# Where VectorE's and GpSimd's instructions stand in a stretch of 128 slots: a rotary embedding kernel

## The chip, the cores and the metric

The kernel runs on one core of one Trainium2 chip. The metric is device time in microseconds for one launch. Three runs gave a median of 163.52 us (163.49 to 163.62). One more execution was taken by the hardware profiler, and all durations below come from that one.

A core has five engines, each with its own stream of instructions: TensorE (PE in the profile; its weight loads are PEld), VectorE (DVE), ScalarE (ACT), GpSimd (POOL) and SyncE (SP). Data moves between the main memory (HBM) and the on-chip memory by 16 DMA engines. In this kernel SP and ACT issue the data transfers; each transfer is split over all 16 DMA engines. The engines' own instructions are also fetched from HBM by these DMA engines; the profile lists such fetches as a queue of kind "instruction".

## The reference

`x` has the shape 8 x 2048 x 8 x 64 (batch, position, head, features), in float32. `cos` and `sin` have one row of 32 values for each position.

```python
x1 = x[..., : x.shape[-1] // 2]
x2 = x[..., x.shape[-1] // 2 :]
out1 = x1 * cos - x2 * sin
out2 = x1 * sin + x2 * cos
return np.concatenate([out1, out2], axis=-1)
```

The input has 33.55 MB and so has the output; each is moved once.

## The kernel before

**Tiling.** A batch is one tile `xt` of 128 partitions with 8192 floats each (16 positions of 512 floats for each partition; 4 MB). Five such tiles exist (`NBUF`), and a result is written into the tile that its input came from. A batch is worked off in pieces of 2048 floats for each partition (`UNIT`); the first and the last batch have some pieces of 1024.

**The work on a piece.** `rotate` knows three kinds. Kind A, most of them: GpSimd makes `t2`, which is x with its halves exchanged, times `sin` for one half and times `-sin` for the other (two instructions, L124); VectorE makes `t1` = x times `cos` (L131) and adds the two into `xt` (L138). In kinds B and C, five pieces in all, TensorE adds by multiplying with a unit matrix `eye` (or its negative `neye`), and ScalarE copies the sum from PSUM into `xt` (L147, L167); in kind C VectorE also does GpSimd's multiplication (L150).

**Transfers.** SP issues the loads of `x` and `cos` (L67, L69) and the stores of the last batch; ACT issues the load of `sin` (L76) and the other stores (L74). The first batch comes in three loads: 1 MB, 1 MB and 2 MB. Five batches are requested at the start; batch b + 5 is requested when batch b has been worked off, and waits for the store that frees the tile.

**The start.** Every engine has a fixed opening of the runtime, then a common barrier. After it VectorE's first own instruction is the copy of `cos` into PSUM (L95), which waits for `cos`. GpSimd's first are a memset and a select that build `eye` (L82, L83); its first multiplication (L124) waits for `sin` and for the first load of `x`. ACT makes `nsin`, the negative of `sin`, the copy `sin_ps` and `neye` (L92 to L94).

**Slots.** An instruction takes one slot of 64 bytes, so 128 slots are 8192 bytes, the size of each larger fetch in the trace. `addr_align(128, offset=k)` is no instruction of the engine: when the program is loaded, it is replaced by as many padding slots as bring the next instruction onto slot k of a stretch of 128. By default the engine walks through the padding, which is empty instructions (NOP); with `max_nops=0` the first padding slot is a jump to the aligned instruction. `keep` fixes an instruction's place in the engine's order. The two calls stand behind the loads and ahead of the building of `eye`. VectorE's 107 instructions from L95 to its last sum (waits that stand alone included) and GpSimd's 78 from L82 to its last product follow.

Of the kernel before, what the change touches and what calls it, by code (L numbers as in the profile page):

```python
# [10 lines left out]
def kernel(  # L11
# [7 lines left out]
    nc = tc.nc  # L19
    keep = tc.keep_in_program_order  # L20
# [56 lines left out]
    for b in range(NBUF):  # L77
        load(b)

    keep(nc.vector.addr_align(128))  # L80
    keep(nc.gpsimd.addr_align(128, offset=120))
    keep(nc.gpsimd.memset(eye, 0.0))  # L82
    nc.gpsimd.affine_select(  # L83
        out=eye,
# [141 lines left out]
```

## Time and profile before

| | |
|---|---|
| median of three runs | 163.52 us (163.49 to 163.62) |
| profiled execution: its own time | 163.48 us |
| profiled execution: span from the first to the last instruction of the program | 161.7 us |
| VectorE busy | 140.1 us, 87% |
| GpSimd busy | 138.8 us, 86% |
| TensorE, ScalarE busy | 49.6 us, 12.8 us |
| moved by DMA | 67.65 MB, 418 GB/s over the span |
| fetches of instructions in the span | 2 |

Times in all views count from the first instruction of the program. What lies between the span and the execution's own time, 1.8 us, is mostly the runtime's closing work. Busy time of an engine excludes the instructions that only wait, branch, pad or issue transfers. A "releaser" is what ended an idle stretch of an engine.

### The profile page before, as it was taken

The numbers are of one execution on the slowest core, as the hardware profiler recorded it, in microseconds if no ns is written. First come the engines' busy times: TensorE is split into PE (matmuls) and PEld (weight loads), VectorE is DVE, ScalarE is ACT, GpSimd is POOL, SyncE is SP. The second block draws the span as 40 slices with busy tenths as digits, with TensorE's granted clock in tenths as the row PEclk, the third lists the DMA queues.
The fourth block names the chain that finished last, engine by engine and source line by source line (L and its number), as shares of the span: only waits on it lengthen the run. The fifth ranks groups of instructions, "written<-read, shape, count | busy, mean of one in ns | idle before, by whom it ended". The sixth has DMA issues, their size and how long they took to land.

```text
span 161.7 us, 573 instructions
## 1 busy us (share of the span) xinstructions
PE 49.6 (31%) x80; PEld 18.7 (12%) x80; DVE 140.1 (87%) x66; ACT 12.8 (8%) x14; POOL 138.8 (86%) x70
## 2 busy tenths in 40 slices
PE   0000000597309760978049723973000000000000
PEld 0000000142004220322023302320000000000000
DVE  0297999999999999999999999199989999899950
ACT  3300000002200220021100220022000000000000
POOL 1399994999999999992999979999799997999800
PEclk9999999999975998589956995599655555555555
DMA  5999999999999999999999999999999999999995
GB/s 184 418 432 438 420 428 405 444 409 489 397 401 450 438 462 397 438 462 397 438 462 397 438 462 397 438 470 389 438 470 389 438 470 397 430 470 397 405 420 213
DMA packets 3458, 67.65 MB, mean 418 GB/s; under 512 B 384, under 2 KB 384, under 8 KB 768
## 3 DMA queue, kind: packets, MB, share of 16 engines
q1 hardware_dynamic: 2016, 38.01, 55.4%
q10 hardware_dynamic: 1440, 29.62, 42.7%
q14 instruction: 2, 0.02, 0.0%
HBM read 34.08 MB, written 33.55 MB: 418 GB/s over the span
## 4 chain that ended last, share of the span: by engine, by line
DMA 48%; DVE 37%; POOL 9%; issue 2%; DVEq 0%; SPq 0%; POOLq 0%; ACTq 0%
DMA xt<-in_x_dram 26%; DMA out_dram<-xt 19%; DVE t L131 18%; DVE xt L138 17%; POOL t L124 9%; DMA sin_sb<-in_sin_dram 4%; DVE t L150 1%; DVEq L138 0%; SPq L67 0%; POOLq L124 0%; ACTq L74 0%
## 5 line engine op out<-in xcount | busy, mean ns | idle before, releaser
L124 POOL TENSOR_TENSOR t<-xt,sin_sb 128x1024 f32<-128x1024 f32 (+1 forms) x32 | 70.5, 2203 | 11.3 <-DMA xt<-in_x_dram 5.2
L131 DVE TENSOR_TENSOR t<-xt,cos_ps 128x2048 f32<-128x2048 f32 (+1 forms) x34 | 73.4, 2167 | 0.8
L124 POOL TENSOR_TENSOR t<-xt,nsin 128x1024 f32<-128x1024 f32 (+1 forms) x32 | 70.5, 2202 | 0.0
L138 DVE TENSOR_TENSOR xt<-t,t 128x2048 f32<-128x2048 f32 (+1 forms) x29 | 62.2, 2145 | 8.0 <-POOL t L124 5.4
L145 PE MATMUL o<-t,eye 128*128 128x512 f32 x24 | 17.2, 807 | 22.9 <-DVE t L131 19.5
L162 PE MATMUL o<-t,eye 128*128 128x512 f32 x16 | 12.1, 847 | 37.7 <-DVE t L131 35.5
L146 PE MATMUL o<-t,eye 128*128 128x512 f32 x24 | 14.9, 709 | 0.0
L147 ACT COPY xt<-o 128x1024 f32<-128x1024 f32 x6 | 6.1, 1012 | 45.7 <-PE o L146 45.7
L145 PEld LDWEIGHTS o<-t,eye 128*128 128x128 f32 x24 | 5.6, 257 | 32.3 <-issue 26.4
L162 PEld LDWEIGHTS o<-t,eye 128*128 128x128 f32 x16 | 3.7, 256 | 43.1 <-issue 39.3
L167 ACT COPY xt<-o 128x1024 f32<-128x1024 f32 x4 | 4.0, 1012 | 47.8 <-PE o L163 36.8
L95 DVE COPY cos_ps<-cos_sb 128x512 f32<-128x512 f32 x1 | 0.7, 695 | 6.9 <-DMA cos_sb<-in_cos_dram 6.9
L146 PEld LDWEIGHTS o<-t,eye 128*128 128x128 f32 x24 | 5.7, 239 | 8.2 <-issue 7.7
L163 PE MATMUL o<-t,neye 128*128 128x512 f32 x8 | 6.3, 882 | 0.2 <-DVE t L150 0.2
L150 DVE TENSOR_TENSOR t<-xt,sin_ps 128x2048 f32<-128x2048 f32 x2 | 4.6, 2281 | 0.0
L163 PE MATMUL o<-t,eye 128*128 128x512 f32 x8 | 4.1, 592 | 0.0
L163 PEld LDWEIGHTS o<-t,neye 128*128 128x128 f32 x8 | 2.2, 306 | 5.3 <-issue 3.7
L82 POOL MEMSET eye<- 128x128 f32 x1 | 0.2, 204 | 2.4 <-issue 2.4
L163 PEld LDWEIGHTS o<-t,eye 128*128 128x128 f32 x8 | 1.5, 190 | 1.9 <-issue 1.9
L92 ACT ACT_TABLE_LOAD x1 | 1.3, 1283 | 1.2 <-PEq L210 1.2
L92 ACT ACTIVATE nsin<-sin_sb 128x512 f32<-128x512 f32 x1 | 0.6, 629 | 4.0 <-DMA sin_sb<-in_sin_dram 4.0
L93 ACT COPY sin_ps<-sin_sb 128x512 f32<-128x512 f32 x1 | 0.6, 579 | 0.0
(6 smaller groups left out, 1.0 us busy)
## 6 DMA issues: line engine op xcount, KB each, us to landing
xt<-in_x_dram SPq DMA_DIRECT2D x7, 4096.0 KB, 41.4
out_dram<-xt ACTq DMA_DIRECT2D x6, 4096.0 KB, 28.6
xt<-in_x_dram SPq DMA_DIRECT2D x2, 1024.0 KB, 6.9
xt<-in_x_dram SPq DMA_DIRECT2D x1, 2048.0 KB, 13.1
out_dram<-xt ACTq DMA_DIRECT2D x1, 2048.0 KB, 25.8
out_dram<-xt SPq DMA_DIRECT2D x1, 2048.0 KB, 10.0
out_dram<-xt SPq DMA_DIRECT2D x2, 1024.0 KB, 6.3
out_dram<-xt ACTq DMA_DIRECT2D x1, 1536.0 KB, 20.7
```

Source lines behind the costliest of these rows:

```text
L92: keep(nc.scalar.mul(nsin, sin_sb, -1.0))
L95: keep(nc.vector.tensor_copy(cos_ps, cos_sb))
L124: nc.gpsimd.tensor_mul(out=t2u[:, :, u, :].rearrange("p (r h) d -> p r h d", h=H), in0=xu[:, :, 1 - u, :].rearrange("p (r h) d -> p r h d" ...
L131: nc.vector.tensor_mul(out=t1.rearrange("p (r k d) -> p r k d", r=nr, d=Dh), in0=xk, in1=rep(cos_ps[:, r0 : r0 + nr, :], 2 * H),)
L138: keep(nc.vector.tensor_add(out=xt, in0=t1, in1=t2))
L145: nc.tensor.matmul(oc, eye, t1[:, cs], start=True, stop=False)
L146: nc.tensor.matmul(oc, eye, t2[:, cs], start=False, stop=True)
L147: keep(nc.scalar.copy(xt[:, 2 * j * C : 2 * (j + 1) * C], o))
L150: nc.vector.tensor_mul(out=t2.rearrange("p (r k d) -> p r k d", r=nr, d=Dh), in0=xk, in1=rep(sin_ps[:, r0 : r0 + nr, :], 2 * H),)
L162: nc.tensor.matmul(oc, eye, t1u[:, gs, u, :], start=True, stop=False)
L163: nc.tensor.matmul(oc, eye if u else neye, t2u[:, gs, 1 - u, :], start=False, stop=True)
L167: nc.scalar.copy(xu[:, :, u, :], o.rearrange("p (g d) -> p g d", d=Dh))
```

## The change

VectorE's and GpSimd's alignment both become slot 8 of a stretch, with a jump in place of the padding's empty instructions. Before, VectorE's copy of `cos` stood on slot 0 and GpSimd's memset of `eye` on slot 120 of a stretch. Nothing else of the program differs: all five engines have the same instructions in the same order with the same waits.

```diff
-    keep(nc.vector.addr_align(128))
-    keep(nc.gpsimd.addr_align(128, offset=120))
+    for eng in (nc.vector, nc.gpsimd):
+        keep(eng.addr_align(128, offset=8, max_nops=0))
     keep(nc.gpsimd.memset(eye, 0.0))
```

## The prediction

> **What bounds the kernel now.** I read the strips of the page first, then a table by stages, then how the run ends.
>
> ```profile
> DVE  0297999999999999999999999199989999899950
> ...
> POOL 1399994999999999992999979999799997999800
> ...
> DMA  5999999999999999999999999999999999999995
> ```
>
> VectorE and GpSimd look full, but each has slices of 1 to 7 tenths; the DMA strip has none between its ends. The table by stages (columns: stretch, its length, busy time of PE, PEld, DVE, ACT, POOL, clock, share of the 16 DMA engines, GB/s) says the same in numbers: from 2 us on the share is 0.96 to 1.02.
>
> ```profile
> 0.00:2.00 2.00, 0.00 (x0) 0.00 (x0) 0.00 (x0) 0.84 (x1) 0.20 (x4) 1.00 0.31 49
> 2.00:8.00 6.00, 0.00 (x0) 0.00 (x0) 1.06 (x2) 1.80 (x4) 2.00 (x4) 1.00 0.96 381
> 8.00:16.00 8.00, 0.00 (x0) 0.00 (x0) 6.84 (x6) 0.00 (x0) 8.00 (x6) 1.00 1.02 434
> ...
> 120.00:158.00 38.00, 0.00 (x0) 0.00 (x0) 34.25 (x17) 0.00 (x0) 31.77 (x16) 0.50 0.99 425
> ```
>
> The trace also records every packet. On one DMA engine a packet starts 3 ns before the one ahead of it ends, so 16 chains of packets can be followed from 1.75 us to the end; they hardly have a hole. They end between 159.41 and 160.50 us. The last store shows it from outside: its 1 MB would take 2.5 us at 424 GB/s (16 packets of 32 KB in 1.213 us each, the usual row), but it was issued at 155.86 and landed at 160.83, 5.0 us later, behind the store before it. So the end is set by the DMA engine that has the most to do. A transfer counts as landed when its slowest DMA engine is through, so one late engine makes everything late, and time of VectorE or GpSimd is worth nothing unless the DMA engines run dry.
>
> **What the padding costs now.** These are the padding and what follows it on both engines.
>
> ```profile
> L80 DVEq NOP  x61: 18/18/18, 0.8 to 3.6; - x61
> L81 POOLq NOP  x52: 13/13/13, 0.7 to 2.7; - x52
> ```
> ```profile
> 2.81 0.20 POOL L82 MEMSET eye<- 128x128 f32 x1 [2.37 <-issue]
> 3.09 0.29 POOL L83 TENSOR_SCALAR_AFFINE_SELECT eye<-eye 128x128 f32<-128x128 f32 x1
> ...
> 6.49 1.26 POOL L124 TENSOR_TENSOR t<-xt,sin_sb 128x512 f32<-128x512 f32 x1 [3.11 <-DMA sin_sb<-in_sin_dram]
> 6.91 0.69 DVE L95 COPY cos_ps<-cos_sb 128x512 f32<-128x512 f32 x1 [6.91 <-DMA cos_sb<-in_cos_dram]
> ...
> 7.49 0.30 ACT L94 ACTIVATE neye<-eye 128x128 f32<-128x128 f32 x1
> ```
>
> VectorE walks 61 slots from 0.76 to 3.62 us (47 ns each), GpSimd 52 from 0.69 to 2.77 us (40 ns each). That is 2.86 and 2.08 us, and none of it counts: VectorE then waits until 6.91 for `cos`, GpSimd until 6.49 for `sin` (3.11 us of waiting left), and `eye`, complete at 3.39, is first read at 7.49, when ACT reaches it. `cos` and `sin` were requested by SP and ACT at 1.17 and 0.73, which wait for neither padding. So taking the empty instructions out: 0. The jump that replaces them has no row here. Its cost is bounded by nothing and by 3.1 us, GpSimd's remaining wait, before it could show; the nearest row is a padding slot, 0.04 to 0.05 us. I take 0. [...]
>
> **What moves: the fetches.** Counting the padding back, VectorE's first padding slot was slot 67 (128 - 61) and GpSimd's 68 (120 - 52). Before, VectorE walks into the next stretch at 3.6 us, with the copy of `cos` on its slot 0. GpSimd has memset, a register move, two configurations, select, one wait and two multiplications on slots 120 to 127, and goes over with its third multiplication. After, both jump there at about 0.75 us and stand on slot 8. From there VectorE's 107 instructions end at slot 114 and GpSimd's 78 at slot 85, so neither crosses again in the program. The two fetches of the page fit these two crossings:
>
> ```profile
> q14 instruction: 2, 0.02, 0.0%
> ```
>
> The packet records put them at 7.688 and 10.466 us, 8192 bytes and 309 ns each, on two DMA engines. Neither came out free: the next packet on the first of these chains took 924 ns where its neighbours take 309, on the second 926 where they take 611. So they cost their DMA engines 0.309 + 0.615 = 0.92 and 0.309 + 0.315 = 0.62 us. The landings show what that does to everyone. Of the 16 parts of the first three loads the last landed 0.13 to 0.15 us after the last but one. Of the second load of `x` (the first one that a fetch hit) it was 0.64, of the third 0.45, and of the last five stores 0.46, 0.42, 0.47, 0.48 and 0.47. The chains end the same way: the last three at 159.999, 160.047 and 160.501. Chains that run in step can be confused in following them, so that the last one is the engine hit at 7.688 is inferred from this steady lag, not read.
>
> What a fetch costs when it comes elsewhere: if it is through before the chains begin at 1.75 us, nothing; inside the stream, 0.62 to 0.92 by the two rows above.
>
> When will they come? VectorE stood on slot 0 from 3.6 to 6.9 us and no fetch came; one came 0.8 us after the copy was released. So the fetch follows not arriving in a stretch but having moved a slot or a few into it. GpSimd got past its first two slots at about 7.15 us (after `nsin` at 7.08) and past the next two at 10.0 (the second load); with 7.688 for VectorE and 10.466 for GpSimd the fetch comes 0.4 to 0.8 us after slot 1 to 3. If what counts is how far into the stretch the engine stands, slot 8 is past the mark at once: both fetches come at 0.75 + 0.4 to 0.8 = 1.15 to 1.55 us, and with 0.31 us for the packet end at 1.5 to 1.9, at the edge of the stream. I take 0 for each there.
>
> **Sum.** Taken away: the delay on both hit chains; the end becomes that of the next chain, 159.999 in place of 160.501: -0.50 us (not -0.92, as the other 14 engines are not helped). Padding 0, jump 0. The execution's 163.48 becomes 162.98; it lies 0.04 under the median of 163.52, so 163.02 us. If only the first-hit engine is freed, the end is 160.047: -0.45, 163.07. If only the other is freed, 0.
>
> [...]
>
> **Rivals.**
> *No change.* VectorE's copy on slot 8 waits for `cos` just as it did on slot 0. If an engine must complete an instruction in the new stretch, jump or not, VectorE's fetch stays at 7.7 us and its DMA engine stays last: 163.5. For it: no fetch in the 3.3 us of standing on slot 0. Against it: slot 8 is deeper in than any mark that fits the two times. The same time results if both fetches land between 2 and 6 us.
> *Slower: the jump breaks the sequence of fetches.* Each engine then fetches the stretch it jumps into and the one after it. One of the two is inside the stream anyway, and a second one there adds 0.62 to 0.92 us on the same DMA engine: 164.1 to 164.4. For it: the trace has no jump to learn from. Against it: before, no engine fetched anything between -8.1 and 7.69 us, though VectorE ran an instruction on slot 1 at 6.92, so its next stretch was there already. It decides from a second fetch after 1.75 us. [...]
> *Slower at the end.* If the jump skips the fetch of the stretch after, an engine that crosses once more in the closing work must wait for it: VectorE ends 8 slots deeper than before. A wait of a fetch's 0.4 to 0.8 us plus 0.31, less the 0.50 gained, is +0.2 to +0.6: 163.7 to 164.1.
>
> **Chances.** Faster as summed (both fetches early, or the one that matters): 0.55. No change: 0.22. Slower by the broken sequence 0.13, at the end 0.10. A difference under 0.2% (0.33 us) can hardly be told from none. The likeliest case alone spans 162.85 (the remaining chains also ending as early as the next ones, 159.85) to 163.2 (a fetch that overlaps the first packets by its 0.3 us). The range goes from 162.85 to 164.1, which takes in no change and the lower part of the slower cases.
>
> **What will show it.** The padding's rows vanish and the memset of `eye` starts near 0.8 us; the first multiplication stays at 6.5 and the copy at 6.9. Packets of kind "instruction" move to before 1.8 us, none lies between 2 and 160. The lag of the last landing falls from 0.47 to about 0.15 us, and the last store lands near 160.3. I am wrong if a fetch still sits at 7.7, if there are more than two, or if the lag stays though the fetches moved: then that DMA engine is late for another reason.

## The result and the profile after

The changed kernel takes 163.85 us (median of 22 runs), the kernel before 163.42 us (22 runs beside it). The ratio is 1.0024, 95% interval 1.0017 to 1.0032: about 0.4 us slower. I had forecast 0.5 us faster. The time lies in the range, on the other side of no change. Executions that ran clearly longer than the others of their kernel (two of the changed kernel's, 167.93 and 170.95 us) enter no ratio and no mean over the runs, and the packet times of e4 and f2 below come from profiled executions of that sort (209.99 and 170.50 us).

The padding and the start of the program in the profile after (columns as before):

```profile
L81 POOLq COMPARE_BRANCH  x1: 33/33/33, 0.7 to 0.7; - x1
L81 DVEq COMPARE_BRANCH  x1: 47/47/47, 0.8 to 0.8; - x1
```
```profile
1.15 0.20 POOL L82 MEMSET eye<- 128x128 f32 x1 [0.70 <-POOLq L210]
...
7.42 1.27 POOL L124 TENSOR_TENSOR t<-xt,sin_sb 128x512 f32<-128x512 f32 x1 [5.71 <-DMA sin_sb<-in_sin_dram]
7.83 0.69 DVE L95 COPY cos_ps<-cos_sb 128x512 f32<-128x512 f32 x1 [7.83 <-DMA cos_sb<-in_cos_dram]
...
8.42 0.30 ACT L94 ACTIVATE neye<-eye 128x128 f32<-128x128 f32 x1
```

The 61 and 52 empty instructions are gone, and the rows of the jumps last 47 and 33 ns. That is not all that a jump takes: `eye` is begun at 1.15 us in place of 2.81, and not near 0.8 as I had expected. Without padding or jump (b1 below) it is begun at 0.73, after a jump inside the stretch (a1) at 0.88. So the jump into the next stretch took GpSimd about 0.4 us, which its wait for `sin` hides. But the first multiplication starts at 7.42 in place of 6.49 and the copy of `cos` at 7.83 in place of 6.91: `sin` and `cos` land 0.93 us later. The strip and the queue line of the page:

```profile
DMA  5999999999999999999999999999999999999995
...
q14 instruction: 2, 0.02, 0.0%
```

The DMA engines are as full as before and there are two instruction packets, as before. (Nothing in the profile tells where they are read from: the 34.08 MB that both pages count as read from HBM are `x`, `cos` and `sin` to the byte.) The packet records have them at 3.012 and 3.474 us (before: 7.688 and 10.466). They came much earlier, and still inside the stream of data, which begins at 1.74 us. The data packets that start as they end took 509 and 878 ns where their neighbours take 309, so the two DMA engines lost 0.5 and 0.9 us. The 16 parts of two transfers land as follows (sorted, us; from the semaphore updates of the DMA engines; the middle ones are left out):

```
               first   8th     14th    15th    16th
before  cos     6.50    6.62    6.72    6.75    6.88
        last    159.76  160.16  160.33  160.36  160.83
after   cos     6.35    6.80    7.00    7.46    7.81
        last    159.72  160.27  160.41  160.68  160.96
```

After, two parts of `cos` land 0.5 and 0.8 us behind the others, and two are still behind when the last store lands. The late start of the multiplications itself is not what costs. VectorE's last sum starts a microsecond earlier than before (the line of before, then that of after):

```profile
154.61 1.23 DVE L138 TENSOR_TENSOR xt<-t,t 128x1024 f32<-128x1024 f32 x1
```
```profile
153.54 1.23 DVE L138 TENSOR_TENSOR xt<-t,t 128x1024 f32<-128x1024 f32 x1
```

SP issues the last store at 154.79 in place of 155.86 us, and it lands 0.13 us later all the same. The DMA engines set the end.

The span of the profiled execution is 161.79 us, 0.12 more than before. The execution's own time is 163.86, 0.38 more. So a part of the loss lies outside the span. Each run gives its time and its span; over the runs, time less span is 2.07 us for the changed kernel. For the kernel before it is 1.81 in the profiled execution and 1.79 to 1.81 on average in each of the five sets of runs beside the experiments. The mean span is 161.80 us against 161.59 to 161.74. So 0.27 us of the loss come after the span (or ahead of it), and 0.1 to 0.2 in it.

### The profile page after: what moved, and what is told of

Read it like the earlier page. It is cut to its first block, busy times and chain, and to the rows that moved or that the text cites. A ratio compares the mean times of both kernels' runs of the same rounds, so it can differ in the third digit from the quotient of the medians.

```text
span 161.8 us, 462 instructions
## 1 busy us (share of the span) xinstructions
PE 48.6 (30%) x80; PEld 18.3 (11%) x80; DVE 140.1 (87%) x66; ACT 12.8 (8%) x14; POOL 138.9 (86%) x70
## 3 DMA queue, kind: packets, MB, share of 16 engines
HBM read 34.08 MB, written 33.55 MB: 418 GB/s over the span
## 4 chain that ended last, share of the span: by engine, by line
DMA 47%; DVE 37%; POOL 9%; issue 2%; DVEq 0%; SPq 0%; POOLq 0%; ACTq 0%
DMA xt<-in_x_dram 24%; DMA out_dram<-xt 18%; DVE t L131 18%; DVE xt L138 17%; POOL t L124 9%; DMA sin_sb<-in_sin_dram 4%; DVE t L150 1%; DVEq L138 0%; SPq L67 0%; POOLq L124 0%; ACTq L74 0%
## 5 line engine op out<-in xcount | busy, mean ns | idle before, releaser
L145 PE MATMUL o<-t,eye 128*128 128x512 f32 x24 | 16.6, 779 | 23.5 <-DVE t L131 20.1
L162 PE MATMUL o<-t,eye 128*128 128x512 f32 x16 | 11.8, 829 | 38.8 <-DVE t L131 36.6
L146 PE MATMUL o<-t,eye 128*128 128x512 f32 x24 | 14.9, 709 | 0.0
L163 PE MATMUL o<-t,eye 128*128 128x512 f32 x8 | 4.1, 592 | 0.0
```

What stands on the lines that cost most here:

```text
L145: nc.tensor.matmul(oc, eye, t1[:, cs], start=True, stop=False)
L146: nc.tensor.matmul(oc, eye, t2[:, cs], start=False, stop=True)
L162: nc.tensor.matmul(oc, eye, t1u[:, gs, u, :], start=True, stop=False)
L163: nc.tensor.matmul(oc, eye if u else neye, t2u[:, gs, 1 - u, :], start=False, stop=True)
```

## The experiments

Four theories were on the table at the start. The *closing theory*: what the change costs lies in the runtime's closing work on VectorE, because its program ends eight slots later. The *early-fetch theory*: the loss comes from the fetches among the first loads. The *depth theory* is the prediction's own rule, that a fetch follows from having moved some slots into a stretch; the *arrival theory* says that it is asked for on arrival and its packet takes microseconds to come.

### Slots and jumps taken apart

Each kernel differs from the kernel before in the two alignment lines alone.

```diff
 a1_jump_old_slots
+    keep(nc.vector.addr_align(128, max_nops=0))
+    keep(nc.gpsimd.addr_align(128, offset=120, max_nops=0))
 a2_new_slots_walked
+    for eng in (nc.vector, nc.gpsimd):
+        keep(eng.addr_align(128, offset=8))
 a3_vector_only
+    keep(nc.vector.addr_align(128, offset=8, max_nops=0))
+    keep(nc.gpsimd.addr_align(128, offset=120))
 a4_gpsimd_only
+    keep(nc.vector.addr_align(128))
+    keep(nc.gpsimd.addr_align(128, offset=8, max_nops=0))
```

> The jump alone: both engines jump, but to the old slots (VectorE 0, GpSimd 120). Arrival theory (a fetch is asked for when the engine arrives in the next stretch and its packet comes 2 to 4 us later): VectorE arrives at 0.8 us, so its packet comes at 3.0 to 3.5 us; GpSimd arrives with its third multiplication as before, so the other stays near 10.5 us. cos and sin come late by one hit DMA engine, 0.3 to 0.6 us instead of 0.93. Closing theory (the 0.25 us that the changed kernel loses outside the span belong to where the streams end): both streams end on the old slots, so execution time less span is 1.8 us as before, and the time lies at most 0.15 us from before. Depth theory of the prediction (a fetch needs an instruction completed in the new stretch): VectorE's packet stays at 7.7 us, time as before.

> The slots alone: both engines on slot 8, walking through the padding (69 slots of 47 ns on VectorE, 68 of 40 ns on GpSimd). Arrival theory: VectorE arrives at 3.6 us as before, its packet stays near 7.7 us; GpSimd arrives at 3.1 us, its packet comes at 5.5 to 7 us in place of 10.5. sin and cos land within 0.3 us of before. Closing theory: streams end on the new slots, so execution time less span is 2.05 us as in the changed kernel, and the time is 0.2 to 0.4 us above before. Depth theory: VectorE stands on slot 8 at 4.0 us, so its packet comes at 4.4 to 4.8 us.

> VectorE alone as in the changed kernel, GpSimd as before. Arrival theory: one packet at 3.0 to 3.5 us, the other at 10.5 us. Closing theory: execution time less span is 2.05 us if VectorE's end slot matters, 1.8 us if GpSimd's does. If the whole loss comes from the early fetches instead, this kernel has about half of the 0.43 us.

> GpSimd alone as in the changed kernel, VectorE as before. Arrival theory: one packet at 3.0 to 3.5 us, the other at 7.7 us. Closing theory: execution time less span is 1.8 us if VectorE's end slot matters, 2.05 us if GpSimd's does. If the whole loss comes from the early fetches instead, this kernel has about half of the 0.43 us.

Measured (ratio to the kernel before; time less span as a mean over the runs; packets from the records):

```
                       ratio, 95% interval       time less span   instruction packets at
a1 jump, old slots     1.0006 (0.9995-1.0017)    1.82             3.76, 10.96
a2 new slots, walked   1.0017 (1.0008-1.0026)    2.03             7.03, 7.24
a3 VectorE only        1.0021 (1.0013-1.0030)    2.05             3.71, 10.85
a4 GpSimd only         0.9995 (0.9986-1.0004)    1.80             1.74, 7.83
```

Three things follow. First, what costs is VectorE's slot 8, however it is reached: the three kernels with it (the changed one, a2, a3) have 2.03 to 2.07 us outside the span and are slower; GpSimd's part of the change costs nothing that can be seen (a4), and the jump alone is within 0.2% of before.

Second, the depth theory is wrong. In a1 VectorE stands on slot 0 just as before and waits for `cos` until 7.76 us, and yet its packet came at 3.76:

```profile
7.76 0.69 DVE L95 COPY cos_ps<-cos_sb 128x512 f32<-128x512 f32 x1 [7.76 <-DMA cos_sb<-in_cos_dram]
```

In a2 VectorE passed slot 8 at 4.4 us, the end of its padding here, and the packets came at 7.03 and 7.24:

```profile
L81 DVEq NOP  x69: 18/18/18, 0.8 to 4.4; - x69
L81 POOLq NOP  x68: 13/13/13, 0.7 to 3.7; - x68
```

A packet follows the arrival in the stretch, and the time between is long and varies. In a4 a jump at 0.7 us on GpSimd gave a packet at 1.74, as the stream of data was only beginning; one at 0.8 on VectorE (a1, a3) gave 3.7 to 3.8, when it had begun; arrivals at 3.1 and 3.6 us (a2) gave 7.0 and 7.2. That is 1.0 us without traffic and 3 to 4 us with it. The changed kernel lies between: its packets came 2.3 and 2.7 us after the jumps, if the first one is GpSimd's. GpSimd's part of it is that of a4, and in c4, d1 and e1 below, where GpSimd jumps at the same time, its packet came at 1.74 to 1.77 too. Why it was not among the first in the profiled execution of the changed kernel, no record shows.

Third, a1 and a3 tell whose packet is whose: what moved with VectorE's jump is the packet that was at 7.69, so that one was VectorE's and the one at 10.47 GpSimd's.

### How the closing time goes with the slot

Again only the alignment differs. In the four that move VectorE, GpSimd stays as before; in c4 VectorE does.

```diff
 c1_vector_slot4, d3_vector_slot12, c2_vector_slot16, c3_vector_slot100
+    keep(nc.vector.addr_align(128, offset=4))     # 12, 16, 100
 c4_gpsimd_slot40
+    keep(nc.gpsimd.addr_align(128, offset=40, max_nops=0))
```

> VectorE on slot 4, walked to; GpSimd as before. What is read is execution time less span: 1.80 us with VectorE on slot 0, 2.03 to 2.07 on slot 8 so far. Step theory (VectorE's closing work goes over the end of its stretch once the program ends late enough in it, and that costs one fixed wait): 1.80 or 2.05, nothing between. Slope theory (the closing work grows by 30 ns for each slot that the program ends later): 1.92. The span stays within 0.1 us of before under both.

> VectorE on slot 16, walked to; GpSimd as before. Step theory: execution time less span 2.05 us, as on slot 8. Slope theory: 2.28 us.

> VectorE on slot 100 of the stretch that it starts in (33 slots of padding, walked); it goes over into the next stretch with its 29th instruction, near 41 us, and its program ends near slot 83, far from an end. GpSimd as before. Step theory: execution time less span 1.80 us. If even the kernel before pays a crossing in the closing work, it is 1.55. Slope theory gives no more than 1.80 either (the program ends earlier in its stretch), near 1.0 if the slope holds all the way. One instruction packet moves from 7.7 to 42 to 46 us; if a fetch among 32 KB packets costs its DMA engine more than one among small ones, the span grows, by 0.3 to 0.6 us.

> GpSimd on slot 40, jumped to, so that its program ends as near to the end of a stretch as VectorE's does on slot 8 to 16; VectorE as before. If any engine's closing work pays for the crossing: execution time less span 2.05 us. If only VectorE's does (GpSimd's is not the last to be done): 1.80 us.

> VectorE on slot 12, walked to; GpSimd as before. Slots 0 and 4 and 16 gave 1.80 us of execution time less span, slot 8 gave 2.05. If only the last few instructions of the closing work pay for going over (earlier ones are covered by waiting for other engines): 1.80 us here too, time as before. If a broad window pays: 2.05 us, time 0.15% above before.

```
                       ratio, 95% interval       time less span
VectorE slot 4   c1    1.0002 (0.9993-1.0012)    1.79
VectorE slot 12  d3    1.0008 (0.9997-1.0019)    1.86
VectorE slot 16  c2    1.0002 (0.9993-1.0011)    1.80
VectorE slot 100 c3    0.9997 (0.9985-1.0008)    1.80
GpSimd slot 40   c4    1.0012 (1.0002-1.0022)    2.03
```

Neither of the two shapes that I had written down holds. It is no slope, and no step that stays: slot 4 is free, slot 8 costs 0.22 to 0.27 us, slot 12 some 0.07, slot 16 nothing (c2; in d1 below, 0.07). It is a window. c4 shows that it is not VectorE's alone: GpSimd, free on slot 8, costs 0.23 us on slot 40, which brings its end near the end of a stretch too. There the trace also shows where: of the semaphore updates by which the engines meet in the closing work, the sequence that stood at 0.64 and 0.68 us after the span's end before stands at 0.64 and 0.92, and all that follows is 0.24 later; a third 8192-byte packet comes at 163.42 us. On slot 16 VectorE has such a packet at 162.83, 1.17 us after the span's end, and loses nothing (d1: 163.41, 1.47 us after it). So the closing work goes over the end of a stretch in these kernels. That its cost depends on whether the engine would have waited for others at that point is my inference. The order of the late updates fits it: the nearer to the stretch's end the program ends, the earlier in the closing work the first late one comes. On slot 16 it is the sixth update (0.65 us after the span's end for 0.64; in d1 the fourth, 0.56 for 0.52), on slot 12 the 13th (1.76 for 1.70). For slot 8 no record shows the crossing: the changed kernel has no packet after the span and no late update, the last one stands at 1.94 us in it and in the kernel before, and only its time is 0.27 us longer.

### The changed kernel with that part undone

```diff
 e1_vector4_gpsimd8 (d1_vector16_gpsimd8: offset=16)
+    keep(nc.vector.addr_align(128, offset=4, max_nops=0))
+    keep(nc.gpsimd.addr_align(128, offset=8, max_nops=0))
```

> The changed kernel with VectorE on slot 4 in place of 8; both still jump and fetch early. Closing theory: execution time less span 1.80 us in place of 2.07, time 163.45 to 163.65, within 0.1% of before. Rival (the early fetches cost the whole 0.4 us): 163.85.

> The changed kernel with VectorE on slot 16 in place of 8, both by a jump. If the loss is mainly the closing work's crossing (free on slot 16 in the run before, 0.24 us on slot 8): execution time less span 1.80 us, time 163.5 to 163.65, at most 0.1% above before. If it is mainly the early fetches that make sin and cos late: it stays at 163.8 to 163.9.

e1: 163.57 us beside 163.41, ratio 1.0010 (0.9999 to 1.0022), time less span 1.81, packets at 1.74 and 3.46 us. d1: ratio 1.0008 (0.9998 to 1.0018), time less span 1.86, packets at 1.74 and 3.57 us. Moving VectorE by four slots takes more than half of the loss away, with all else of the change in place. What may be left, 0.1% with an interval that includes none, is in the span. The kernels with an early fetch of VectorE (a1, a3, e1, d1) have mean spans 0.05 to 0.12 us over the kernel before, a4, where only GpSimd's is early, 0.05 under it. That would point to VectorE's packet among the first loads. But a2, whose packets came at 7.0 and 7.2 us, is 0.09 over as well, and each of these differences is uncertain by about 0.1 us or more. What makes the part of the loss that lies in the span stays open.

### What a fetch costs in the stream

```diff
 d2_seven_crossings (the kernel before, and in the loop over the batches)
+        if b > 0:
+            keep(nc.vector.addr_align(128, offset=8, max_nops=0))
```

> Before, with VectorE jumping to slot 8 of the next stretch at the start of each of the batches 1 to 7: seven fetches more, on the same DMA engine, at 25 to 140 us. Chain theory (the end is set by the DMA engine with the most to do, and a fetch costs it 0.31 us and 0.3 to 0.6 more in the packet behind it): +4.3 to +6.4 us on that engine, time 167.7 to 170 if it is the last one already, up to 0.5 less if not. If a late DMA engine is made up for by the others, or the fetch's packet is all that it costs: at most +2.2 us, 165.6, or no change.

169.67 us, ratio 1.0379 (1.0365 to 1.0393): 6.2 us more. Nine instruction packets, seven more than before, one for each jump into a next stretch of 128 slots (0.07 MB in nine, so 8192 bytes for 128 slots), and a DMA strip that has holes now; the second fence has the seven jumps:

```profile
DMA  5999998999989999999999999999999999969760
...
q14 instruction: 9, 0.07, 0.1%
```
```profile
L190 DVEq COMPARE_BRANCH  x7: 41/41/53, 25.7 to 137.1; - x7
```

The rows of the jumps last 41 to 53 ns each, and VectorE's next multiplication follows the sum that runs meanwhile without a gap at all seven, so it is not the jumps that cost. The seven packets took 0.31 us each, 2.2 in all, and the packet behind each took 475 to 659 ns more than its like, 4.1 us in all: 6.3 us, within 0.1 of what the kernel lost. The chains of packets show it on one DMA engine alone: fifteen end between 163.53 and 163.70 us and one at 166.70; the last part of the last store lands 3.0 us after the 15th. (The fifteen end later than before as well; the strip has holes where they run dry, and I read these as loads and stores that wait for the late one.) So the bound of the prediction stands: the end follows the DMA engine that has the most to do, and a fetch of VectorE's costs that one 0.8 to 1.0 us among 32 KB packets.

### No alignment at all

```diff
 b1_no_align
-    keep(nc.vector.addr_align(128))
-    keep(nc.gpsimd.addr_align(128, offset=120))
```

> No alignment on either engine: VectorE starts on slot 67 and goes over with its 62nd instruction, near 90 us, GpSimd on 68 and over with its 61st, near 120 us. No instruction packet before 80 us, two between 85 and 125 us. If a fetch costs its DMA engine 0.6 to 0.9 us wherever it comes: time as before within 0.1%, execution time less span 1.80 us (programs end near slots 50 and 27). If fetches among the first loads are what costs: 0.2 to 0.5 us faster.

163.37 us, ratio 0.9999 (0.9990 to 1.0009), time less span 1.80; packets at 96.45 and 118.27 us. Fetches near 100 us cost no more and no less than those near 7.7 and 10.5, as far as can be told, and the old alignment was worth nothing that can be measured.

### Fetches that really come first

To see whether the prediction's saving exists, the first transfers are held back. Padding slots ahead of them do that, since alternating alignments to even and odd slots give one slot each (e3: 11 padding rows on SP and 11 on ACT, from 0.7 to 1.1 us).

```diff
 e2_delay5 (on e1; e3_delay10: range(11); e4_before_delay10: range(11) on the kernel before;
            f1_delay2: range(3); f2_sync_delay5: range(6), nc.sync alone)
+    for eng in (nc.sync, nc.scalar):
+        for k in range(6):
+            keep(eng.addr_align(2, offset=k % 2))
     keep(nc.scalar.dma_start(out=sin_sb, in_=sin_src))
```

> The kernel on VectorE slot 4 and GpSimd slot 8, with 5 or 6 padding slots ahead of the first transfers of SP and ACT (about 0.2 us; the stream starts near 1.95 us). If a fetch that is ahead of the first data packet is free: GpSimd's packet near 1.75 us, VectorE's near 1.8 to 2.0, no lag of a fetch's size in the landings, span about 0.5 us shorter for the fetches and 0.2 longer for the start: 163.1 to 163.3. If VectorE's fetch needs 3 us whatever the DMA engines do: it stays at 3.7 us and the time is 0.2 us above the kernel without the padding.

> The same with 10 or 11 padding slots, about 0.4 us. If free ahead of the stream: both packets before the first data packet (near 2.15 us), time 163.2 to 163.4. If VectorE's fetch needs 3 us anyway: 163.8 to 164.0.

> The control: the kernel before with the same 10 or 11 padding slots ahead of the first transfers. If the DMA engines bound the kernel from the first packet to the last, 0.4 us of late start are 0.4 us of time: 163.85. If there is slack anywhere, less.

> VectorE slot 4, GpSimd slot 8, 2 or 3 padding slots (about 0.1 us) ahead of the first transfers of SP and ACT. If 0.1 us is enough for VectorE's packet to be ahead of the data of its DMA engine (it came at 1.90 us when it was free): packet near 1.9, even landings, 163.2 to 163.3. If not: packet at 3.4 to 3.7 us, 163.6.

> The same with 5 or 6 padding slots on SP alone; sin is requested as early as before. If the first data packets are SP's (they were, in every trace so far): both packets ahead of the data, as with both held back, and sin lands a little earlier; 163.2 to 163.4. If ACT's transfer is then first on VectorE's DMA engine: packet at 3.4 to 3.7 us, 163.6 to 163.8.

```
                       ratio, 95% interval       packets at      first data packet
e2 5-6 slots           1.0001 (0.9988-1.0013)    1.76, 1.90      1.99
e3 10-11 slots         1.0020 (1.0003-1.0036)    1.75, 1.90      2.17
e4 before, 10-11       1.0040 (1.0026-1.0055)    7.31, 10.80     2.16
f1 2-3 slots           0.9998 (0.9984-1.0012)    1.74, 2.05      1.88
f2 5-6, SP alone       0.9997 (0.9988-1.0007)    1.74, 3.07      1.75
```

In e2 both packets are ahead of the first data packet, and VectorE's came 1.1 us after its jump, where in e1, with the data not held back, it took 2.7: so it is the data in the stream that makes it late. The start of the stream in its profile: SP's first transfer is issued at 0.97 us in place of 0.74, and yet the first multiplication comes at 6.68, where the changed kernel had 7.42.

```profile
0.97 0.38 SPq L67 DMA_DIRECT2D xt<-in_x_dram  x1
...
6.68 1.26 POOL L127 TENSOR_TENSOR t<-xt,sin_sb 128x512 f32<-128x512 f32 x1 [4.96 <-DMA sin_sb<-in_sin_dram]
```

The last part of `cos` lands 0.04 us after the last but one (before: 0.13), of the last store 0.12 (before: 0.47): no DMA engine is behind any more. e3 against its control e4, both with the same late start: 163.58 against 164.01 us, 0.4 less (0.3 by the means, with an interval of about 0.1 to 0.6 us from 12 and 6 runs). So fetches ahead of the stream do save something, about 0.3 to 0.4 us. But to get there the start has to wait: e2 pays 0.2 us for it and ends where the kernel before is. e2 and e3 both came out slower than I had expected (163.1 to 163.3 and 163.2 to 163.4 us). A shorter wait (f1) and one of SP alone (f2) gave nothing to be told from no change either; VectorE's packet was behind the first data packet in both. None of the 18 kernels is measurably faster than the kernel before. The control e4 lost 0.6 us by the medians to the kernel before, more than the 0.4 us by which its start is late; the interval of its ratio, 0.4 to 0.9 us, takes in both.

## Why the prediction was wrong, point by point

*What bounds the kernel*: right. (One number beside it was off: 16 packets of 32 KB in 1.213 us are 432 GB/s, not 424, and the last store 2.4 us, not 2.5; nothing hangs on it.) The DMA engine with the most to do sets the end; seven more fetches on it cost 6.2 us against 6.3 by their packets' own rows. The later start of all the arithmetic by 0.93 us cost little or nothing, as stores that were issued a microsecond earlier did not land earlier.

*The padding and the jump at 0*: right. 2.86 and 2.08 us of empty instructions left without a trace in the time, and so did the jumps. But a jump is no padding slot in size: GpSimd's took about 0.4 us and not 0.04, and the wait for `sin` covered it.

*When the fetches come*: this is the step that failed. I had read the 3.3 us in which VectorE stood on slot 0 without a packet as "the fetch follows not arriving in a stretch but having moved a slot or a few into it", and from there took 0.4 to 0.8 us from trigger to packet. The same rows fit an arrival at 3.6 us and 4 us until the packet, and GpSimd's an arrival near 7.15 and 3.3 us; I didn't consider a delay that long. a1 and a2 separate the two readings. With 2.3 to 2.7 us from the jump to the packet, both fetches fell on the stream's first loads, and nothing of the 0.50 us was saved. The fetch that the sum needed out of the way is VectorE's, and that one came at 3.5 to 3.8 us in every kernel with VectorE's jump and the old start; GpSimd's alone came as early as 1.74 us, at the edge of the stream, in four others. That they came ahead of `sin` and `cos` moved the first product 0.93 us back as well.

*What a fetch ahead of the stream is worth*: the size was near. -0.50 us was the sum; e3 against e4 has 0.3 to 0.4, with the start held back in both.

*A fetch inside the stream*: 0.62 to 0.92 us by the two rows of before; 0.79 to 0.97 in d2. It fell on the data and not on the engine that fetches: past the start, the waits of VectorE and GpSimd in the profile after are for data and for each other (GpSimd 6.1 us for `xt`, VectorE 3.4 us for GpSimd's products), and at the seven jumps of d2 VectorE's next multiplication follows without a gap.

*The rivals*: the third one, "slower at the end", is what happened, with a chance of 0.10. Its place was right (VectorE's closing work, eight slots deeper), its price was not: 0.7 to 1.1 us for a fetch waited for, less 0.50 saved; measured 0.27, with nothing saved. I gave it as a consequence of a skipped fetch. By what slots 12 and 16 and c4 show, the end of a stretch in the closing work is enough; that it costs most where nothing else is waited for is inferred. "No change" by fetches that land between 2 and 6 us was named too and holds for the span, within 0.1 to 0.2 us. "The jump breaks the sequence of fetches" fell: two packets, not four. (That no engine fetched anything from -8.1 us on holds for packets of 8192 bytes; five of 40 bytes and of the same kind stand between -0.8 and 0 us.)

## What to carry to other kernels

When DMA engines bound a kernel, look at the landings of single DMA engines. Here one part of the last store lagged 0.47 us behind the other 15 before the change, and 3.0 us in d2, and the DMA engine of that part set the end. A small transfer of another kind on that one (here instructions, 8 KB for 0.8 to 1.0 us each in d2) cost its full time: 6.2 us for seven, against 6.3 by their packets' rows. An instant at which nothing happens does not show that nothing was asked for (here 1.0 to 4.8 us lay between the arrival in a stretch and its packet); before taking a trigger from a trace, list every event earlier than it that could be the cause, however long the delay. And compare time and span separately: here eight slots in front of VectorE's program cost 0.22 to 0.27 us outside the span, and no row of the span shows it.

## What the runs showed of the hardware that I had not expected

- An instruction packet came 1.0 to 1.1 us after the engine's arrival in the next stretch when the DMA engines were idle (a4, e2), and 2.3 to 4.8 us after it when they were busy (the changed kernel; d2: jumps from 25.7 to 137.1 us, packets from 29.98 to 141.62).
- The data packet behind an instruction packet took 0.2 to 0.66 us longer than its like in nearly every case in the stream (0.62 and 0.32 in the kernel before, 0.20 and 0.57 in the changed one, 0.48 to 0.66 in d2), so that 309 ns of fetch cost about 0.5 to 1.0 us.
- The row of a jump (33 ns on GpSimd) tells little of its cost: the next instruction came about 0.15 us later than without a jump when it stayed in its stretch (a1), about 0.4 us later when it went to the next one (a4, the changed kernel).
- Eight slots more in front of VectorE's program changed the time less span from 1.80 us to between 2.03 and 2.07 (a2, a3, the changed kernel), and four more slots took most of that away again (1.86, d3).
